# The banded attention of a hybrid encoder block: softmax issued behind the turned queries' copy in early slots, and a bank for transposed probabilities taken from the projections' ring

## The chip, the core and the metric

One core of a Trainium2 chip runs the whole kernel. TensorE (PE) does matrix products and transposes, ScalarE (ACT) activations and copies, VectorE (DVE) elementwise work and reductions, SyncE (SP) issues the DMAs. The metric is the device time of one execution in microseconds. Times of several executions are given by their median; the profile is of one further execution.

## What is computed

One encoder block on x of 1024 tokens and 1024 features, all in fp32. The change lies in branch B, attention within a window of 128 tokens, in blocks of 128 queries, 8 query heads on 2 key/value heads:

```python
h = rms_norm(x)
g_q, g_k, g_v, g_r, g_lr_f, g_lr_b, s_q, s_k, s_v, gate_a, gate_b = split(h @ w_in)
y_gla = gla_branch(...) @ w_o_gla                  # branch A, gated linear attention
q = rope(rms_norm(s_q)); k = rope(rms_norm(s_k))   # branch B
scores = q @ k.T * hd**-0.5, masked to |i - j| <= 128
m = maximum(scores.max(-1), sink)
p = exp(scores - m)
o = (p / (p.sum(-1) + exp(sink - m))) @ v
y_swa = o @ w_o_swa
x = x + (sigmoid(gate_a) * y_gla + sigmoid(gate_b) * y_swa) @ w_out
x = x + swiglu(rms_norm(x))
```

## The kernel before

A product in fp32 is made of three products of split operands (`mm3`, L73): each operand is a rounded high part and the rest, and high x high, high x low and low x high are summed in PSUM. So each operand has a copy on ACT (the high part, `...h`) and a subtraction on DVE (the low part, `...l`).

The kernel has three stretches: the first projections with the gated linear attention (to some 380 us), the banded attention beside projections (some 380 to 570 us), and the large products of the output and the feed-forward part (to the end, on PE almost alone). The change touches the second.

The second stretch runs in 22 time slots. The list `todo` gives each slot its stages; a unit n is one block of 128 queries of one key/value head (four query heads), 16 in all. The unit is prepared and rotated (`prep`, `a_rope`) around slot n+1, its queries are turned (`a_turn`) in slot n+2, scored in slot n+3 (`a_scores`, once for each of four heads), its probabilities transposed and split in slot n+4 (`a_probs`, for up to three key blocks) and multiplied with the values in slot n+5 (`a_out`). Within a slot the order is prep, a_rope, a_scores, a_turn, k_turn, a_out, a_probs. So slot t does the scores of unit t-3 and the turn of unit t-2, whose scores come in slot t+1.

`slot` emits the stages one after another, and after each it lets generators in the list `dense` emit a share of matmuls of other work (`fill`): first the projections (L73 with `wh`, `wl` and `xh`, `xl`; four accumulators at a time, whose results ACT scales and stores, L221 and L222), and, when these are used up, the first halves of later products (L246; two accumulators, which DVE scales, L249). When only the latter is left, `len(dense)` is 1.

PE runs in the order in which the code is written. The order on ACT, DVE and SP is set by a scheduler from the order in which instructions are emitted and from what they depend on; each of these queues then runs strictly in its order. PSUM has eight banks: four in the ring `mm` (`mmtile`: accumulators of projections and first halves) and four in the ring `ch` (`chtile`: scores, transposes, attention outputs). A tile of a ring takes the bank that was freed first, and its first writer waits until the last reader of that bank is done.

The steps that matter, by line: transposed queries `ch<-ident,qr` (L755), their copy `sqh` on ACT (L758) and rest `sql` on DVE (L759); scores `ch<-kTh,sqh` and the like (L73), with the mask and the row maximum on DVE (`p`, `mx`, L773); the softmax, which is emitted with the fourth head's scores: `mx`, `nm`, `es` on DVE (L780, L781, L783), `es` on ACT (L784), four exponentials on ACT (L787), `dn` and `rd` on DVE (L789, L791), four scales on ACT (L793); transposed probabilities `ch<-ident,p` (L804) with copy `ph` on ACT (L807) and rest `pl` on DVE (L808); the output copy `st<-ch` on ACT (L818), which four DMAs store (L820). Loads: `qr<-sq` (L716) and `kvr<-skv` (L722) on SP; `kvr` feeds the products of the key rotation on DVE (L695 to L698) and the values' split `vSh`, `vSl` (L731, L732).

Of the kernel before, what the change touches and what calls it, by code (L numbers as in the profile page):

```python
# [11 lines left out]
AF = mybir.ActivationFunctionType  # L12
ALU = mybir.AluOpType

P = 128
# [9 lines left out]
SF = ((2, 50), (9, 24), (18, 18), (1 << 30, 12))  # L25
# [5 lines left out]
def body(tc, i, out):  # L31
    nc = tc.nc
    with ExitStack() as root:
# [8 lines left out]
        def nm(s):  # L42
            uid[0] += 1
            return f"{s}_{uid[0]}"
# [4 lines left out]
        def chtile(shape, dt=F32):  # L49
            return psc.tile(list(shape), dt, tag="ch", name=nm("ch"))  # L50
# [24 lines left out]
        def mm3(o, ah, al, bh, bl, start, stop):  # L75
            mm(o, ah, bh, start, False)
            mm(o, ah, bl, False, False)
            mm(o, al, bh, False, stop)
# [177 lines left out]
        dense = []  # L256

        def fill(n):

            while n > 0 and dense:  # L260
                try:
                    next(dense[0])
                    n -= 1
                except StopIteration:
                    dense.pop(0)

        def share(plan, t):
            return next(n for end, n in plan if t < end)
# [5 lines left out]
        def slot(stages, n):  # L274

            stages = [f for f in stages if f]
            done = 0
            if not stages:
                fill(n)
            for j, f in enumerate(stages):  # L280
                f()
                t = n * (j + 1) // len(stages)
                fill(t - done)
                done = t
# [361 lines left out]
        with tc.manual_schedule(engines={mybir.EngineType.PE}):  # L646
            fill(44)
            for t in range(last + 1):
                work = [[at[t, j]] for j in (0, 5, 4, 3, 2, 1) if (t, j) in at]
                if t in behind:  # L650
                    work = work or [[]]
# [38 lines left out]
        keys, att = {}, {}  # L690
# [60 lines left out]
        def a_turn(g, n):  # L751
            a = att[g, n]
            qt = chtile((P, 4, P))
            for h in range(4):
                nc.tensor.transpose(qt[:, h], a.qn[:, h], ident)  # L755
            a.qh = sw.tile([P, 4, P], FR, tag="qh", name=nm("sqh"))
            a.ql = sw.tile([P, 4, P], FR, tag="ql", name=nm("sql"))
            nc.scalar.activation(a.qh, qt, AF.Copy)  # L758
            nc.vector.tensor_tensor(a.ql, qt, a.qh.bitcast(F32), op=ALU.subtract)  # L759
            a.b0, a.b1 = max(n - 1, 0), min(n + 1, KT - 1)  # L760
            a.w = (a.b1 - a.b0 + 1) * P

        def a_scores(g, n, h):
            a = att[g, n]
            if h == 0:
                a.p = sw.tile([P, 4, 384], F32, tag="p", name=nm("p"))
                a.mx = sw.tile([P, 4], F32, tag="mx", name=nm("mx"))
            w, p, mx = a.w, a.p, a.mx
            ks = slice(a.b0 * P, (a.b1 + 1) * P)
            mo = (a.b0 - (n - 1)) * P  # L770
            s = chtile((P, 384))
            mm3(s[:, :w], a.qh[:, h], a.ql[:, h], kTh[:, g, ks], kTl[:, g, ks], True, True)
            nc.vector.tensor_tensor_reduce(out=p[:, h, :w], in0=s[:, :w], in1=band[:, mo:mo + w],  # L773
                                           op0=ALU.add, op1=ALU.max, scale=1.0, scalar=-1e30,
                                           accum_out=mx[:, h:h + 1])
            if h < 3:
                return
            sk = sink[:, 4 * g:4 * g + 4]
            nm_ = sw.tile([P, 4], F32, tag="nm", name=nm("nm"))
            nc.vector.scalar_tensor_tensor(mx, mx, -1.0, a.rs, op0=ALU.mult, op1=ALU.mult)  # L780
            nc.vector.tensor_tensor(nm_, mx, nsink[:, 4 * g:4 * g + 4], op=ALU.min)  # L781
            es = sw.tile([P, 4], F32, tag="es", name=nm("es"))
            nc.vector.tensor_tensor(es, sk, nm_, op=ALU.add)  # L783
            nc.scalar.activation(es, es, AF.Exp)  # L784
            dn = sw.tile([P, 4], F32, tag="dn", name=nm("dn"))
            for h in range(4):
                nc.scalar.activation(p[:, h, :w], p[:, h, :w], AF.Exp, bias=nm_[:, h:h + 1],  # L787
                                     scale=a.rs[:, h:h + 1], accum_out=dn[:, h:h + 1])
            nc.vector.tensor_tensor(dn, dn, es, op=ALU.add)  # L789
            rd = sw.tile([P, 4], F32, tag="rd", name=nm("rd"))  # L790
            nc.vector.reciprocal(rd, dn)  # L791
            for h in range(4):
                nc.scalar.activation(p[:, h, :w], p[:, h, :w], AF.Copy, scale=rd[:, h:h + 1])  # L793

        def a_probs(g, n, kb):
            a = att[g, n]
            kb += a.b0
            if kb > a.b1:
                return
            if kb == a.b0:  # L800
                a.pts = []
            pt = chtile((P, 4, P))
            for h in range(4):
                nc.tensor.transpose(pt[:, h], a.p[:, h, (kb - a.b0) * P:(kb - a.b0 + 1) * P], ident)  # L804
            ph = sw.tile([P, 4, P], FR, tag="ph", name=nm("ph"), bufs=3)
            pl = sw.tile([P, 4, P], FR, tag="pl", name=nm("pl"), bufs=3)
            nc.scalar.activation(ph, pt, AF.Copy)  # L807
            nc.vector.tensor_tensor(pl, pt, ph.bitcast(F32), op=ALU.subtract)  # L808
            a.pts.append((kb, ph, pl))
# [24 lines left out]
        def xpart(q, k):  # L834
            r = xn.tile([P, HT], F32, tag="xn", name=nm("xn"))
            nc.sync.dma_start(out=r, in_=scr[f"x{q}", k])
            pool, th, tl, d = homes[q]
            XT[q].append(xsplit(pool, th.format(k + d), tl.format(k + d), r))
# [4 lines left out]
        for n in range(2 * KT):  # L843
            t, g = divmod(n, 2)
            todo[n + 5].append((a_out, g, t))
            todo[n + 4] += [(a_probs, g, t, kb) for kb in range(3)]
            todo[n + 3] += [(a_scores, g, t, h) for h in range(4)]
            todo[n + 2].append((a_turn, g, t))
            todo[n + 1].append((a_rope, g, t))
            if g == 0:  # L850
                todo[n + 1].append((prep, t))
                if t + 1 < KT:
                    todo[n + 2].append((k_turn, t + 1))
        order = (prep, a_rope, a_scores, a_turn, k_turn, a_out, a_probs)
        with tc.manual_schedule(engines={mybir.EngineType.PE}):
            for t, v in enumerate(todo):
                v.sort(key=lambda e: order.index(e[0]))
                if t > 2 * KT + 2 and v:
                    fill(8)
                slot([lambda e=e: e[0](*e[1:]) for e in v], share(SF, t))  # L860
                if t >= 2 * KT + 2:
                    assert len(dense) == 1
                    for q in ("T1", "22"):
                        xpart(q, t - 2 * KT - 2)
# [81 lines left out]
        def pair_T3(f):  # L946
            nme, m, a, b = PAIRS[f]
            g = pend[f]
            product(g.X, wsplit(g.s3, 512), XT["T3"], 4, False, True)
            return result((f"{nme}{m + 4}", 1), g.X, g.p5)  # L950
# [69 lines left out]
        with tc.manual_schedule(engines={mybir.EngineType.PE}):  # L1020
# [15 lines left out]
            for j in range(0, len(PAIRS), 2):  # L1036
# [4 lines left out]
                v = [pair_T3(f) for f in two]  # L1041
# [53 lines left out]
        def gate(nme, s):  # L1095
            g = bt.tile([P, HT], F32, tag=nme[:2], name=nm(nme[:2]))
            nc.sync.dma_start(out=g, in_=scr[nme, s])
            nc.scalar.activation(g, g, AF.Sigmoid)
            return g
# [119 lines left out]
        with tc.manual_schedule(engines={mybir.EngineType.PE}):  # L1219
# [29 lines left out]
            for m in (0, 4, 1, 5, 2, 6, 3, 7):  # L1249
                g = [gate(f"gb{m}", s) for s in range(2)]  # L1250
# [353 lines left out]
```

## Time and profile before

| | |
|---|---|
| median of three executions | 1626.66 us (1625.54 to 1628.33) |
| profiled execution | 1624.41 us |
| its span (first to last instruction) | 1622.6 us |
| PE busy | 1610.2 us (99%) |
| PE weight loads busy | 1339.9 us (83%) |
| DVE busy | 1222.0 us (75%) |
| ACT busy | 914.1 us (56%) |
| DMA | 323.26 MB, 198 GB/s over the span |

"Busy" is the share of the span in which an engine had an instruction running. PE's matmuls overlap, so their starts tell more than their lengths: where nothing holds PE, 512 columns follow each other every 0.23 us. In a timeline a row has the start and the duration in us, the engine, the line of the kernel, the operation, tiles written and read, and in brackets how long the engine stood idle before the row and which instruction released it.

### The profile page before, as it was taken

The page shows a single profiled execution, that of the slowest core. Times are in us where ns is not written, and L with a number is a line of the kernel's source. Part 1 is how long each engine was busy: PE and PEld are TensorE (multiplying, and loading weights), DVE is VectorE, ACT ScalarE, POOL GpSimd, SP SyncE. Part 2 cuts the span into 40 slices and gives each one's busy share as a digit, 9 for nine tenths or more (in the row PEclk, how much of TensorE's full clock was granted, in tenths as well). Part 3 has the DMA queues.
Part 4 walks back from the last instruction along what each step waited for, and adds up shares of the span by engine and source line. Part 5 has one row for each costly group of instructions (what it writes and reads, how often), then busy time and mean ns, then how long its engine had stood idle before and what let it go on. Part 6 is the DMA issues. An engine that isn't in the chain of part 4 may idle for free.

```text
span 1622.6 us, 23346 instructions
## 1 busy us (share of the span) xinstructions
PE 1610.2 (99%) x7628; PEld 1339.9 (83%) x7628; DVE 1222.0 (75%) x2307; ACT 914.1 (56%) x1875; POOL 0.2 (0%) x4
## 2 busy tenths in 40 slices
PE   9999999999999999999999999999999999999999
PEld 6888888888788888888888888888888888888887
DVE  8568888846899777876855878677777887789655
ACT  7455777863999745455633647754444444454442
POOL 0000000000000000000000000000000000000000
PEclk9999999999999999999999999999999999999999
DMA  8955757878554387878843656643435564695433
GB/s 272 306 180 187 254 191 242 274 264 279 170 173 143 105 283 257 271 237 261 286 120 95 192 196 210 196 141 123 137 120 178 168 220 145 209 332 186 149 98 117
DMA packets 197980, 323.26 MB, mean 199 GB/s; under 512 B 23423, under 2 KB 49919, under 8 KB 197858
## 3 DMA queue, kind: packets, MB, share of 16 engines
q1 hardware_dynamic: 197858, 321.77, 60.8%
q8 instruction: 60, 0.98, 0.3%
q14 instruction: 62, 0.51, 0.1%
HBM read 216.29 MB, written 105.39 MB: 198 GB/s over the span
## 4 chain that ended last, share of the span: by engine, by line
PE 85%; DVE 8%; ACT 4%; DMA 2%; issue 1%; SPq 0%; DVEq 0%; ACTq 0%
PE mm L73 16%; PE mm L898 10%; PE mm L900 10%; PE mm L899 10%; PE mm L1442 7%; PE ch L1442 6%; PE ch L898 5%; PE ch L900 5%; PE ch L899 5%; PE ch L73 5%; PE mm L246 4%; PE ch L804 1%; DMA kvr<-skv 1%; DVE wl L69 1%; DVE G L443 0%
## 5 line engine op out<-in xcount | busy, mean ns | idle before, releaser
L877 ACT ACTIVATE wh<-ws 128x512 fp32r<-128x512 f32 x164 | 103.1, 630 | 165.4 <-PE mm L899 85.8
L73 PE MATMUL mm<-wh,xl 128*128 128x512 f32 x320 | 127.2, 397 | 0.0
L73 PE MATMUL mm<-wl,xh 128*128 128x512 f32 x320 | 127.1, 397 | 0.0
L73 PE MATMUL mm<-wh,xh 128*128 128x512 f32 x320 | 126.6, 396 | 0.3 <-ACT lrt L313 0.3
L878 DVE TENSOR_TENSOR wl<-ws,wh 128x512 fp32r<-128x512 f32 x164 | 112.1, 685 | 15.4 <-ACT wh L877 14.9
L67 ACT ACTIVATE wh<-wr 128x512 fp32r<-128x512 f32 x114 | 70.8, 627 | 52.8 <-PE mm L73 20.0
L69 DVE TENSOR_TENSOR wl<-wr,wh 128x512 fp32r<-128x512 f32 x114 | 77.7, 684 | 22.5 <-ACT wh L67 21.3
L877 ACT ACTIVATE wh<-a 128x512 fp32r<-128x512 f32 x66 | 41.6, 632 | 89.6 <-PE ch L1442 42.3
L877 ACT ACTIVATE wh<-wr 128x512 fp32r<-128x512 f32 x76 | 48.0, 632 | 61.1 <-PE mm L899 19.9
L878 DVE TENSOR_TENSOR wl<-a,wh 128x512 fp32r<-128x512 f32 x66 | 45.3, 688 | 39.7 <-ACT wh L877 39.5
L73 PEld LDWEIGHTS mm<-wh,xh 128*128 128x128 f32 x320 | 60.2, 188 | 10.6 <-ACT lrt L313 0.7
L1442 PE MATMUL mm<-hh,wl 128*128 128x512 f32 x176 | 68.6, 390 | 0.0
L1442 PE MATMUL mm<-hh,wh 128*128 128x512 f32 x176 | 68.5, 389 | 0.0
L1442 PE MATMUL mm<-hl,wh 128*128 128x512 f32 x176 | 68.5, 389 | 0.0
L73 PEld LDWEIGHTS mm<-wl,xh 128*128 128x128 f32 x320 | 60.2, 188 | 9.7
L73 PEld LDWEIGHTS mm<-wh,xl 128*128 128x128 f32 x320 | 60.3, 188 | 9.0
L891 DVE TENSOR_TENSOR ws<-wr,wr 128x512 f32<-128x512 f32 x80 | 54.4, 684 | 7.1 <-DMA wr<-in_w_f_dram 3.2
L878 DVE TENSOR_TENSOR wl<-wr,wh 128x512 fp32r<-128x512 f32 x76 | 51.8, 683 | 7.0 <-ACT wh L877 6.4
L1409 DVE TENSOR_TENSOR hl<-hr,hh 128x512 fp32r<-128x512 f32 x77 | 52.6, 683 | 5.5 <-ACT hh L1408 5.4
L1408 ACT ACTIVATE hh<-hr 128x512 fp32r<-128x512 f32 x77 | 47.7, 619 | 8.5 <-DMA hr<-B 4.5
L73 PE MATMUL mm<-xl,wh 128*128 128x512 f32 x128 | 50.7, 396 | 0.7 <-DVE xl L330 0.7
L1442 PE MATMUL ch<-hh,wl 128*128 128x512 f32 x132 | 51.4, 389 | 0.0
(453 smaller groups left out, 4982.1 us busy)
## 6 DMA issues: line engine op xcount, KB each, us to landing
wr<-in_w_fi_dram SPq DMA_DIRECT2D x110, 256.0 KB, 3.8
wr<-in_w_f_dram SPq DMA_DIRECT2D x96, 256.0 KB, 3.5
wh<-wh SPq DMA_DIRECT2D x80, 256.0 KB, 3.0
wl<-wl SPq DMA_DIRECT2D x80, 256.0 KB, 3.1
B<-c SPq DMA_DIRECT2D x44, 256.0 KB, 2.1
T<-st SPq DMA_DIRECT2D x44, 256.0 KB, 2.9
a<-in_w_fo_dram SPq DMA_DIRECT2D x44, 256.0 KB, 5.3
hr<-T SPq DMA_DIRECT2D x44, 256.0 KB, 2.6
```

The costliest lines, as they stand in the source:

```text
L67: nc.scalar.activation(h, raw, AF.Copy)
L69: nc.vector.tensor_tensor(l, raw, h.bitcast(F32), op=ALU.subtract)
L73: nc.tensor.matmul(o, a, b, start=start, stop=stop)
L246: nc.tensor.matmul(Y[q], w[:, c], x, start=f0, stop=f1, skip_group_check=True)
L877: nc.scalar.activation(h, src, AF.Copy)
L878: nc.vector.tensor_tensor(l, src, h.bitcast(F32), op=ALU.subtract)
L891: nc.vector.tensor_tensor(t, x, y, op=op)
L898: nc.tensor.matmul(o, h[:, c], x[kk][0], start=start and kk == 0, stop=False, skip_group_check=True)
L899: nc.tensor.matmul(o, h[:, c], x[kk][1], start=False, stop=False, skip_group_check=True)
L900: nc.tensor.matmul(o, l[:, c], x[kk][0], start=False, stop=kk == nk - 1, skip_group_check=True)
L1409: nc.vector.tensor_tensor(l, r, h.bitcast(F32), op=ALU.subtract)
L1442: nc.tensor.matmul(ys[m], a[:, c], b, start=f0, stop=f1, skip_group_check=True)
```

## The change

Two edits. The first takes the softmax out of `a_scores` and emits it as a step of its own (`a_soft`, `a_exps`): in slots below 5 that also turn queries, behind the turn and with `tc.issue_after`, which holds the softmax's instructions behind ACT's copy of those queries (`turned[-1]`); in all other slots directly behind the slot's last scores, where it was. Scores begin in slot 3, so slots 3 and 4 are the ones in which the new place is used. The second edit takes the tile of the first key block's transposed probabilities from the ring `mm` instead of `ch`, as long as only the first halves are left in `dense`; this is so for twelve units. No instruction is added or removed, and PE's order is the same in both kernels but for the bank that those twelve groups write.

```diff
@@ -755,7 +755,7 @@
                 nc.tensor.transpose(qt[:, h], a.qn[:, h], ident)
             a.qh = sw.tile([P, 4, P], FR, tag="qh", name=nm("sqh"))
             a.ql = sw.tile([P, 4, P], FR, tag="ql", name=nm("sql"))
-            nc.scalar.activation(a.qh, qt, AF.Copy)
+            turned.append(nc.scalar.activation(a.qh, qt, AF.Copy))
             nc.vector.tensor_tensor(a.ql, qt, a.qh.bitcast(F32), op=ALU.subtract)
             a.b0, a.b1 = max(n - 1, 0), min(n + 1, KT - 1)
             a.w = (a.b1 - a.b0 + 1) * P
@@ -773,8 +773,16 @@
             nc.vector.tensor_tensor_reduce(out=p[:, h, :w], in0=s[:, :w], in1=band[:, mo:mo + w],
                                            op0=ALU.add, op1=ALU.max, scale=1.0, scalar=-1e30,
                                            accum_out=mx[:, h:h + 1])
-            if h < 3:
-                return
+
+        turned = []
+
+        def a_soft(g, n, pin):
+            a = att[g, n]
+            w, p, mx = a.w, a.p, a.mx
+            with tc.issue_after(turned[-1].ins) if pin else nullcontext():
+                a_exps(a, g, w, p, mx)
+
+        def a_exps(a, g, w, p, mx):
             sk = sink[:, 4 * g:4 * g + 4]
             nm_ = sw.tile([P, 4], F32, tag="nm", name=nm("nm"))
             nc.vector.scalar_tensor_tensor(mx, mx, -1.0, a.rs, op0=ALU.mult, op1=ALU.mult)
@@ -799,7 +807,7 @@
                 return
             if kb == a.b0:
                 a.pts = []
-            pt = chtile((P, 4, P))
+            pt = (mmtile if kb == a.b0 and len(dense) == 1 else chtile)((P, 4, P))
             for h in range(4):
                 nc.tensor.transpose(pt[:, h], a.p[:, h, (kb - a.b0) * P:(kb - a.b0 + 1) * P], ident)
             ph = sw.tile([P, 4, P], FR, tag="ph", name=nm("ph"), bufs=3)
@@ -857,7 +865,14 @@
                 v.sort(key=lambda e: order.index(e[0]))
                 if t > 2 * KT + 2 and v:
                     fill(8)
-                slot([lambda e=e: e[0](*e[1:]) for e in v], share(SF, t))
+                work = [[e] for e in v]
+                names = [e[0] for e in v]
+                if a_scores in names:
+                    pin = a_turn in names and t < 5
+                    k = names.index(a_turn) if pin else max(j for j, f in enumerate(names) if f is a_scores)
+                    g = v[names.index(a_scores)]
+                    work[k].append((a_soft, g[1], g[2], pin))
+                slot([lambda u=u: [f(*a) for f, *a in u] for u in work], share(SF, t))
                 if t >= 2 * KT + 2:
                     assert len(dense) == 1
                     for q in ("T1", "22"):
```

In the changed kernel the lines from L780 on are numbered 8 higher (L787 is L795, L804 is L812), and from the slots' loop on 15 higher. The scheduler's order of ACT and DVE differs in many places between 404 us and 570 us; the three that follow are those of the prediction. Tile names have running numbers.

ACT in slot 3 (`st` is a projection's result, `p` the probabilities of unit 0, `sqh` the copy of unit 1's turned queries that the next scores on PE read):

```order
 L221 ACTIVATE st_5473<-mm_5229,rstdt 128x512
-L787 ACTIVATE p_5401,dn_5448<-p_5401,nm_5442,rs_5201 128x256
-L784 ACTIVATE es_5445<-es_5445 128x4
-L787 ACTIVATE p_5401,dn_5448<-p_5401,nm_5442,rs_5201 128x256 x3
-L758 ACTIVATE sqh_5468<-ch_5463 128x512
+L758 ACTIVATE sqh_5450<-ch_5445 128x512
+L792 ACTIVATE es_5457<-es_5457 128x4
+L795 ACTIVATE p_5401,dn_5460<-p_5401,nm_5454,rs_5201 128x256 x4
 L221 ACTIVATE st_5495<-mm_5230,rstdt 128x512
-L793 ACTIVATE p_5401<-p_5401,rd_5454 128x256 x4
+L801 ACTIVATE p_5401<-p_5401,rd_5466 128x256 x4
```

The copy sqh moved ahead of es and the four exponentials; the next projection's store and the four scales stay behind them.

DVE at the same place:

```order
 L698 TENSOR_TENSOR qn_5615<-qn_5615,sq_5616 128x256
-L695 TENSOR_TENSOR rq_5627<-qr_5598,qB 128x4x64
-L789 TENSOR_TENSOR dn_5448<-dn_5448,es_5445 128x4
-L695 TENSOR_TENSOR rq_5627<-qr_5598,qB 128x4x64
-L791 RECIPROCAL rd_5454<-dn_5448 128x4
-L759 TENSOR_TENSOR sql_5469<-ch_5463,sqh_5468 128x512
+L759 TENSOR_TENSOR sql_5451<-ch_5445,sqh_5450 128x512
 L773 ISA p_5487,mx_5488<-ch_5489,band 128x256
 L773 ISA mx_5488 128x1
```

The split sql moved from behind dn and rd to right behind the key rotation's last row.

DVE where the scores of unit 5 begin (slot 8, around 450 us; `kvr` the loaded keys and values of a later block, `pl` the splits of unit 3's three transposed probabilities), before:

```order
L695 TENSOR_TENSOR sq_6508<-kvr_6494,kB 128x2x64 x2
L773 ISA p_6053,mx_6054<-ch_6055,band 128x384
L773 ISA mx_6054 128x1
L808 TENSOR_TENSOR pl_6014<-ch_6008,ph_6013 128x512
L808 TENSOR_TENSOR pl_6025<-ch_6019,ph_6024 128x512
L808 TENSOR_TENSOR pl_6040<-ch_6034,ph_6039 128x512
L773 ISA p_6053,mx_6054<-ch_6074,band 128x384
```

and after:

```order
L816 TENSOR_TENSOR pl_6014<-ch_6008,ph_6013 128x512
L695 TENSOR_TENSOR sq_6508<-kvr_6494,kB 128x2x64 x2
L773 ISA p_6053,mx_6054<-ch_6055,band 128x384
L773 ISA mx_6054 128x1
L773 ISA p_6053,mx_6054<-ch_6074,band 128x384
L773 ISA mx_6054 128x1
L816 TENSOR_TENSOR pl_6025<-ch_6019,ph_6024 128x512
```

The first pl moved ahead of the two products that read kvr, and the other two behind the second and third scores.

ACT in slot 18 (softmax of unit 15, `st` the output of unit 13, `ph` the copies of unit 14's probabilities), before:

```order
L787 ACTIVATE p_7484,dn_7516<-p_7484,nm_7510,rs_7084 128x256
L784 ACTIVATE es_7513<-es_7513 128x4
L787 ACTIVATE p_7484,dn_7516<-p_7484,nm_7510,rs_7084 128x256 x3
L818 COPY st_7540<-ch_7530 128x512
L807 ACTIVATE ph_7552<-ch_7547 128x512
L807 ACTIVATE ph_7575<-ch_7570 128x512
L793 ACTIVATE p_7484<-p_7484,rd_7522 128x256 x4
```

and after:

```order
L826 COPY st_7540<-ch_7530 128x512
L792 ACTIVATE es_7513<-es_7513 128x4
L795 ACTIVATE p_7484,dn_7516<-p_7484,nm_7510,rs_7084 128x256 x4
L815 ACTIVATE ph_7552<-mm_7547 128x512
L801 ACTIVATE p_7484<-p_7484,rd_7522 128x256 x4
L815 ACTIVATE ph_7575<-ch_7570 128x512
```

The copy st moved ahead of the exponentials, and the four scales between the first and the second ph. The first ph now reads a bank of the ring mm.

## The prediction

> **What bounds the kernel now.** I read the page first, then busy time by stage, then TensorE's waits by stage, and last the timelines around those waits. The page's first and fourth parts:
>
> ```profile
> PE 1610.2 (99%) x7628; PEld 1339.9 (83%) x7628; DVE 1222.0 (75%) x2307; ACT 914.1 (56%) x1875; POOL 0.2 (0%) x4
> ...
> PE 85%; DVE 8%; ACT 4%; DMA 2%; issue 1%; SPq 0%; DVEq 0%; ACTq 0%
> ```
>
> TensorE (PE) is busy 99% of the span and carries 85% of the chain that ended last. An average hides stages, so the same by stretch: window, its length, then busy us (and instructions) of PE, PEld, DVE, ACT and POOL, granted clock, DMA share, GB/s.
>
> ```profile
> 380.00:455.00 75.00, 71.37 (x369) 59.85 (x368) 58.86 (x175) 56.40 (x139) 0.00 (x0) 1.00 0.68 221
> 455.00:572.00 117.00, 116.69 (x633) 98.58 (x632) 101.22 (x280) 100.89 (x246) 0.00 (x0) 1.00 0.43 133
> 572.00:1200.00 628.00, 628.00 (x2771) 519.93 (x2770) 465.93 (x741) 326.01 (x564) 0.00 (x0) 1.00 0.61 197
> ```
>
> The change lies in the first two. From 572 on PE has no idle time at all, and the clock is 1.00, so what PE gains or loses before 572 arrives at the end unchanged. What can be gained is PE's waits there (us in total, times, longest), of the first window and, last row, of the second:
>
> ```profile
> PE ch L73 <- ACT sqh L758: 2.8, 1, 2.8
> PE ch L73 <- DVE mx L773: 0.7, 1, 0.7
> PE ch L73 <- DVE sql L759: 0.2, 1, 0.2
> ...
> PE ch L73 <- DVE mx L773: 0.2, 1, 0.2
> ```
>
> Under 4 us in all, so this is a change of a few us at most.
>
> **Part one, slot 3: the copy of turned queries goes ahead of the exponentials.** PE's, ACT's and DVE's timelines there (start, duration, line, tiles, idle before and its releaser):
>
> ```profile
> 403.31 0.60 PE L755 MATMUL ch<-ident,qr 128*128 128x128 f32 x4
> ...
> 404.68 0.39 PE L73 MATMUL mm<-wl,xh 128*128 128x512 f32 x1
> 404.91 0.40 PE L73 MATMUL mm<-wh,xl 128*128 128x512 f32 x1
> 408.06 0.39 PE L73 MATMUL ch<-kTh,sqh 128*128 128x256 f32 x1 [2.76 <-ACT sqh L758]
> ...
> 408.79 0.39 PE L73 MATMUL ch<-kTh,sql 128*128 128x256 f32 x1 [0.22 <-DVE sql L759]
> ```
>
> ```profile
> 403.82 0.67 ACT L221 ACTIVATE st<-mm,rstdt 128x512 f32<-128x512 f32 x1
> 404.99 0.60 ACT L787 ACTIVATE p<-p,nm,rs 128x256 f32<-128x256 f32 x1 [0.49 <-DVE nm L781]
> ...
> 407.44 0.57 ACT L758 ACTIVATE sqh<-ch 128x512 fp32r<-128x512 f32 x1
> 407.91 0.67 ACT L221 ACTIVATE st<-mm,rstdt 128x512 f32<-128x512 f32 x1
> 408.48 1.70 ACT L793 ACTIVATE p<-p,rd 128x256 f32<-128x256 f32 x4
> ```
>
> ```profile
> 405.21 0.15 DVE L783 TENSOR_TENSOR es<-sink,nm 128x4 f32<-128x4 f32 x1
> 405.28 0.42 DVE L698 TENSOR_TENSOR qn<-qn,sq 128x256 f32<-128x256 f32 x1
> ...
> 408.06 0.67 DVE L759 TENSOR_TENSOR sql<-ch,sqh 128x512 fp32r<-128x512 f32 x1
> ```
>
> The transposes end at 403.91. The copy sqh needs nothing else, yet ACT runs it at 407.44, behind four exponentials that it entered at 404.99. In the changed order it follows the store at 403.82, which holds ACT for 0.57 (407.91 to 408.48, the same form): sqh runs from 404.39 to 404.96. PE would arrive 0.23 after its 404.91 row, at 405.14, so the 2.8 us wait is gone. What is late next is sql on DVE, now behind es and qn: 405.28 + 0.34 (the row pitch of a 0.42 us operation: 0.42 less 0.08 overlap) = 405.62, and 0.67 long, 406.29; PE's third score matmul takes it 0.06 later (408.73 to 408.79 before), at 406.35. Unhindered it would start at 405.14 + 2 x 0.12 = 405.38 (256 columns at half the pitch of 0.23 that the 512-column rows show), so a new wait of about 0.97 appears. Gain: 408.79 - 406.35 = **2.44**. Upper bound, sql not late: 408.79 - 405.38 = 3.41. Lower bound 0: the copy as late as now. A loss in this part is excluded only as far as nothing behind the exponentials is late, and that is next.
>
> The four exponentials and es now start behind sqh and es on DVE (405.36), at 405.5, and end near 407.85; the store of st (L221) then starts at 407.85 against 407.91, and the four scales at 408.4 against 408.48. So they move by nothing on the clock, but PE stands 2.44 earlier. The scales end at 410.2; their reader (L804) stood at 413.95, now 411.5: covered by 1.3. The store's DMA on SP, and the three loads behind it (two weights and kvr), stay where they were:
>
> ```profile
> 410.00 0.38 SPq L722 DMA_DIRECT2D kvr<-skv  x1
> ```
>
> ```profile
> 414.54 0.42 ACT L723 ACTIVATE sq<-kvr 128x256 f32<-128x256 f32 x1 [0.26 <-DMA kvr<-skv]
> ```
>
> On DVE a product of kvr (L695) now stands ahead of the split pl of the first probabilities (L808), whose bank a score of slot 5 takes at 419.6, now 417.1. 414.5 + 0.3 + 0.7 = 415.5: covered by 1.6. I cost this part's other moves, L717 (1.06 us on ACT, now behind exponentials) and the splits of x, at nothing: their readers are the k turns and products several us away.
>
> **Part two, the score at 451.86.** PE's row, and the row before it:
>
> ```profile
> 450.81 0.40 PE L246 MATMUL mm<-xl,wh 128*128 128x512 f32 x1
> 451.86 0.44 PE L73 MATMUL ch<-kTh,sqh 128*128 128x384 f32 x1 [0.65 <-DVE mx L773]
> ```
>
> ```profile
> 450.84 0.49 DVE L695 TENSOR_TENSOR sq<-kvr,kB 128x128 f32<-128x128 f32 x2 [2.17 <-DMA kvr<-skv]
> ```
>
> The score could start at 450.81 + 0.23 = 451.04 and starts 0.82 late; its second matmul loses another 0.10. It waits for a ch bank that DVE frees in order, behind two products that wait 2.17 for kvr. In the new order pl of the first probabilities stands ahead of these products and frees a bank: ACT's copy ph lies before the scales and takes about 0.6, pl 0.7, and it is ready some 0.7 before PE asks. Gain **0.92**. The next score then hangs on mx behind kvr with about 0.3 to spare. Bounds: 0 (kvr 0.8 late or more) to 0.92.
>
> **Part three, the bank from the projections' ring.** From 459 to 566, twelve times, the first block's transposed probabilities no longer take one of the four ch banks. Before, six scores stand late for a ch bank there, the first and the last of them being:
>
> ```profile
> 492.69 0.40 PE L246 MATMUL mm<-xl,wh 128*128 128x512 f32 x1
> 493.00 0.44 PE L73 MATMUL ch<-kTh,sqh 128*128 128x384 f32 x1
> ...
> 546.28 0.40 PE L246 MATMUL mm<-xl,wh 128*128 128x512 f32 x1
> 546.83 0.38 PE L73 MATMUL ch<-kTh,sqh 128*128 128x256 f32 x1 [0.15 <-DVE mx L773]
> ```
>
> With a pitch of 0.23 these are 0.08 and 0.32 late; the others (494.31, 514.98, 535.59, 545.59), read the same way, 0.22, 0.20, 0.14 and 0.23, and each next matmul is 0.08 to 0.10 late too: 1.19 + 0.54 = 1.73. With a bank more, I take **1.65**; bounds 0 and 1.73. The four mm banks bear it: L246 holds two, and two are free.
>
> **Part four, a loss at the end.** ACT's order also changes in the last slots. Slot 18 now (the second fence is PE, at the start of slot 19):
>
> ```profile
> 558.96 0.60 ACT L787 ACTIVATE p<-p,nm,rs 128x256 f32<-128x256 f32 x1 [1.60 <-DVE nm L781]
> ...
> 561.40 0.56 ACT L818 COPY st<-ch 128x512 f32<-128x512 f32 x1
> 561.87 1.07 ACT L807 ACTIVATE ph<-ch 128x512 fp32r<-128x512 f32 x2
> 562.84 1.71 ACT L793 ACTIVATE p<-p,rd 128x256 f32<-128x256 f32 x4
> ```
>
> ```profile
> 559.37 0.39 PE L73 MATMUL ch<-ph,vSl 128*128 128x512 f32 x1
> ...
> 563.71 0.39 PE L73 MATMUL ch<-ph,vSh 128*128 128x512 f32 x1
> 563.94 0.39 PE L73 MATMUL ch<-pl,vSh 128*128 128x512 f32 x1
> ...
> 564.40 0.39 PE L73 MATMUL ch<-ph,vSh 128*128 128x512 f32 x1
> 564.63 0.39 PE L73 MATMUL ch<-pl,vSh 128*128 128x512 f32 x1
> ```
>
> After, the copy st stands first. It waits for the product that ends at 559.76, so the exponentials start at 560.37 instead of 558.96 and end (561.40 - 558.96 = 2.44 long) at 562.81. First ph to 563.38, its pl (0.67) to 564.05, which PE wants at 563.94: late by 0.15. Then the four scales, 1.71, before the second ph: 563.29 + 1.66 + 0.54 = 565.49, wanted at 564.40 + 0.15: late by 0.95. Its pl at 566.2, wanted at 564.63 + 1.10: late by 0.45 to 0.5. Sum 1.6, with 0.1 for the matmul behind a stall **1.7**. Slot 17 has the same new order, and by the same sum just fits (0.25). Bounds: 0 (the scheduler's order runs early because nm is early) and 3.4 (slot 17 too).
>
> **Sum.** -2.44 - 0.92 - 1.65 + 1.7 = -3.3. The profiled execution takes 1624.41, so about 1621.1; it stands 2.25 under the median of the runs, 1626.66, which gives **1623.4**. That is -0.20%, and 0.2% (3.25 us) is about what a measurement of this kernel can tell from no change.
>
> **Rivals.**
> - The tail fits. If slot 18's copies come in time, -5.0: 1621.7. For it: st and exponentials are both short. Against: the sum above leaves over a microsecond.
> - The first wait only changes its name. If DVE's rows ahead of sql stand later than now, or the two thin covers (0.3 at the second place, 0.25 in slot 17) fail, some 2.3 of the gain goes: -1.0, 1625.7. For it: sql is already the last to come in my own sum, and DVE is busy 101.22 of 117.
> - Slower: ACT's new order makes copies late in many slots. The price per slot is the 1.7 of slot 18; gains of 5.0 are used up from the third such slot on, and with four the time is 1626.66 - 5.0 + 6.8 = 1628.5; with five, 1630.2. For it: ACT is busy 100.89 of 117 and PE has no slack. Against: in the printed order only the last two put the scales between the first and the second ph.
> - PE is not the bound. A row for it is PEld, busy only 83%; then the removed waits return as other idle time, and the time stays 1626.7. Against it: PE has 628.00 of 628.00 from 572 on, and its matmuls there follow each other without a gap. [...]
>
> **How the numbers follow.** My sum 0.46 (it ends on the bound: faster 0.25, no difference 0.21); the tail fits 0.20 (faster); the first wait changes its name 0.20 (no difference); many late copies 0.10 (slower 0.08, no difference 0.02); PE not the bound 0.04 (no difference). Faster 0.45, same 0.47, slower 0.08. The range: all waits gone and no loss is -3.41 - 0.92 - 1.73 = -6.1, 1620.6; the upper end takes in the case of no effect, 1626.7, and leaves out the slower rival: 1620.5 to 1626.8.
>
> **What would show it.** In the changed profile the wait of PE for ACT's sqh is absent, a wait of some 0.9 for DVE's sql stands at 406; the wait at 451.86 (then near 448.6) and the small ones at 490 to 547 are gone; and between 558 and 562 PE waits twice or three times for ph and pl, 1.6 in all. I am wrong if sql comes by 405.4, if the late kvr (414.5, 448.2) passes its covers of 1.6 and 0.3, or if ph waits appear in more slots than 18.

## Result and profile after

The changed kernel takes 1621.67 us (median of 9 executions, 1621.26 to 1622.94) against 1626.66 us (9 executions, 1625.29 to 1628.33): ratio 0.9972, 95% interval [0.9962, 0.9982], or 2.9 to 6.2 us less (the ratio is not taken from the two medians, which alone would give 0.9969). Forecast were 1623.4 and -3.3. Its profiled execution took 1621.67, its own median, with a span of 1619.9; before's profiled execution, 1624.41, lay below all nine of its timed ones. Profile against profile the gain is 2.74; median against median 5.0. One later execution of before took 2821.80 us at a mean granted clock of 0.656; it is in no median, ratio or count below.

Page of the changed kernel, busy shares and chain:

```profile
PE 1609.6 (99%) x7628; PEld 1341.0 (83%) x7628; DVE 1223.6 (76%) x2307; ACT 914.7 (56%) x1875; POOL 0.2 (0%) x4
...
PE 90%; DVE 5%; ACT 2%; DMA 1%; issue 1%; SPq 0%; DVEq 0%; ACTq 0%
```

PE's share of the chain reads 90% where it read 85%. That share is no measure of the gain: the fastest variant below, with before's order in slot 18, has 87%. By stretch, and then PE's waits (first row of the first stretch, the others of the second):

```profile
380.00:455.00 75.00, 74.05 (x385) 62.67 (x384) 61.33 (x180) 57.78 (x143) 0.00 (x0) 1.00 0.68 221
455.00:572.00 117.00, 115.90 (x628) 98.43 (x627) 100.57 (x278) 101.58 (x247) 0.00 (x0) 1.00 0.45 139
```

```profile
PE ch L73 <- DVE sql L759: 0.8, 1, 0.8
...
PE ch L73 <- ACT ph L815: 0.8, 1, 0.8
PE ch L73 <- DVE pl L816: 0.2, 1, 0.2
```

PE's idle time before 455 went from 3.6 to 0.95 us; after 455 it went from 0.3 to 1.1. The wait for sqh is gone, one for sql is new, and so are those for ph and pl. Slot 4's first scores on PE, and ACT and DVE at the same place:

```profile
405.34 0.39 PE L73 MATMUL mm<-wh,xl 128*128 128x512 f32 x1
405.57 0.28 PE L73 MATMUL ch<-kTh,sqh 128*128 128x256 f32 x1
405.69 0.28 PE L73 MATMUL ch<-kTl,sqh 128*128 128x256 f32 x1
406.77 0.38 PE L73 MATMUL ch<-kTh,sql 128*128 128x256 f32 x1 [0.81 <-DVE sql L759]
```

```profile
404.70 0.59 ACT L758 ACTIVATE sqh<-ch 128x512 fp32r<-128x512 f32 x1
405.81 0.20 ACT L792 ACTIVATE es<-es 128x4 f32<-128x4 f32 x1 [0.52 <-DVE es L791]
```

```profile
405.70 0.42 DVE L698 TENSOR_TENSOR qn<-qn,sq 128x256 f32<-128x256 f32 x1
406.03 0.68 DVE L759 TENSOR_TENSOR sql<-ch,sqh 128x512 fp32r<-128x512 f32 x1
```

The first two matmuls follow the dense work without a gap; the third could start at 405.69 + 0.12 = 405.81 and comes 0.96 late. The score that stood late at 451.86, in the changed kernel (PE, and DVE's products of kvr):

```profile
448.70 0.39 PE L246 MATMUL mm<-xl,wh 128*128 128x512 f32 x1
448.93 0.33 PE L73 MATMUL ch<-kTh,sqh 128*128 128x384 f32 x1
```

```profile
447.92 0.48 DVE L695 TENSOR_TENSOR sq<-kvr,kB 128x128 f32<-128x128 f32 x2
```

No gap on PE. The end of slot 18, ACT and then PE:

```profile
555.45 0.59 ACT L826 COPY st<-ch 128x512 f32<-128x512 f32 x1 [1.68 <-PE ch L73]
555.93 0.21 ACT L792 ACTIVATE es<-es 128x4 f32<-128x4 f32 x1
556.04 0.59 ACT L795 ACTIVATE p<-p,nm,rs 128x256 f32<-128x256 f32 x1
...
558.38 0.58 ACT L815 ACTIVATE ph<-mm 128x512 fp32r<-128x512 f32 x1
558.98 1.71 ACT L801 ACTIVATE p<-p,rd 128x256 f32<-128x256 f32 x4
560.59 0.57 ACT L815 ACTIVATE ph<-ch 128x512 fp32r<-128x512 f32 x1
```

```profile
559.37 0.40 PE L73 MATMUL ch<-ph,vSh 128*128 128x512 f32 x1
559.74 0.50 PE L73 MATMUL ch<-pl,vSh 128*128 128x512 f32 x1
560.07 0.39 PE L73 MATMUL ch<-ph,vSl 128*128 128x512 f32 x1
561.22 0.49 PE L73 MATMUL ch<-ph,vSh 128*128 128x512 f32 x1 [0.76 <-ACT ph L815]
561.95 0.50 PE L73 MATMUL ch<-pl,vSh 128*128 128x512 f32 x1 [0.23 <-DVE pl L816]
```

With a pitch of 0.23, PE loses 0.14, 0.10, 0.92, 0.50 and 0.10 here: 1.8.

### The profile page after: what moved, and what is told of

Read it like the earlier page. It is cut to its first block, busy times and chain, and to the rows that moved or that the text cites. A ratio compares the mean times of both kernels' runs of the same rounds, so it can differ in the third digit from the quotient of the medians.

```text
span 1619.9 us, 23336 instructions
## 1 busy us (share of the span) xinstructions
PE 1609.6 (99%) x7628; PEld 1341.0 (83%) x7628; DVE 1223.6 (76%) x2307; ACT 914.7 (56%) x1875; POOL 0.2 (0%) x4
## 4 chain that ended last, share of the span: by engine, by line
PE 90%; DVE 5%; ACT 2%; DMA 1%; issue 1%; SPq 0%; DVEq 0%; ACTq 0%
PE mm L73 19%; PE mm L915 10%; PE mm L913 10%; PE mm L914 10%; PE mm L1457 7%; PE ch L73 7%; PE ch L1457 6%; PE ch L915 5%; PE ch L913 5%; PE ch L914 5%; PE mm L246 4%; PE ch L812 1%; DVE wl L69 0%; PE ch L755 0%; DVE G L443 0%
## 5 line engine op out<-in xcount | busy, mean ns | idle before, releaser
L1457 PE MATMUL ch<-hh,wh 128*128 128x512 f32 x132 | 51.3, 389 | 0.0
L1457 PE MATMUL ch<-hl,wh 128*128 128x512 f32 x132 | 51.3, 389 | 0.0
```

Source lines behind the costliest of these rows:

```text
L1457: nc.tensor.matmul(ys[m], a[:, c], b, start=f0, stop=f1, skip_group_check=True)
```

## Experiments

The numbers of the theory come from laying PE's matmuls of two profiles side by side in order, and taking the difference of their starts. Ratios are against executions of before in the same round; its medians in the three rounds were 1626.93, 1626.35 and 1626.70 us. The first four ran together.

**Only the first edit.** `pt = chtile((P, 4, P))` kept, the softmax moved.

```diff
-            pt = (mmtile if kb == a.b0 and len(dense) == 1 else chtile)((P, 4, P))
+            pt = chtile((P, 4, P))
```

> Only the first edit (the softmax behind the turned queries' copy in slots 3 and 4); the transposed probabilities stay in the ring ch. Theory: the two edits add up. The printed order of ACT and DVE up to 455 us is that of the full change, so the wait of 2.9 in slot 3 becomes one of 0.96 for sql (-2.5 with the matmul behind it) and the wait of 0.9 at 451.9 goes: -3.4 us against before, 1623.2; the small waits between 490 and 547 stay, and the 1.8 us of waits in slot 18 are absent. Rival: the measured -5.0 is more than the sum of -3.3 because before loses more in slots 3 to 8 than its one profile shows; then this edit alone gives the whole -5.0, 1621.7.

1621.42 us, ratio 0.9972 [0.9961, 0.9983]: the whole gain. The theory's number (1623.2) was missed, the rival's was met. All six executions lay between 1620.96 and 1622.56.

**Only the second edit.**

```diff
-            pt = chtile((P, 4, P))
+            pt = (mmtile if kb == a.b0 and len(dense) == 1 else chtile)((P, 4, P))
```

> Only the second edit (the first key block's transposed probabilities in the ring mm); the softmax stays where it was. Theory: the small waits for ch banks go (-1.7), and the loss in slot 18 (+1.8) and a wait of 0.36 in slot 18's scores belong to this edit: +0.5 us against before, 1627.1, no difference that can be told. The wait for sqh at 408 (2.9) stays. Rival: the order in slot 18 is the doing of the softmax's new place; then this edit gives -1.7, 1625.0, and no waits for ph in slot 18.

1627.55 us, ratio 1.0004 [0.9996, 1.0013]; waits of PE after 455:

```profile
PE ch L73 <- ACT ph L807: 0.8, 1, 0.8
PE ch L73 <- DVE mx L773: 0.7, 1, 0.7
PE ch L73 <- DVE pl L808: 0.2, 1, 0.2
```

The wait for ph is here without the first edit: the loss in slot 18 belongs to the bank, which takes what it gives. The softmax's new place does not cause it.

**The changed kernel with before's order in slot 18.**

```diff
+            with tc.issue_after(exped[-1].ins) if 2 * n + g in (13,) else nullcontext():
-            nc.scalar.copy(ob, o)
+                nc.scalar.copy(ob, o)
```

(`exped` collects each unit's last exponential.)

> The full change, with ACT's copy of unit 13's output held behind the exponentials of unit 15 in slot 18, which restores before's order there (exponentials, st, ph, ph, then the scales). Theory: the 1.8 us that PE loses in slot 18 for ph and pl are due to that order alone and nothing takes their place: 1.8 under the full change, 1619.9, and no PE wait for ph. Rival: the copies are late for another cause (a busy ACT), or the next wait takes their place: within 0.5 of the full change, 1621.7.

1620.15 us, ratio 0.9964 [0.9952, 0.9977], the fastest median of this study; the interval overlaps that of the full change, so the order of the two rests on the trace. PE there:

```profile
559.21 0.40 PE L73 MATMUL ch<-ph,vSh 128*128 128x512 f32 x1
559.47 0.50 PE L73 MATMUL ch<-pl,vSh 128*128 128x512 f32 x1
559.80 0.40 PE L73 MATMUL ch<-ph,vSl 128*128 128x512 f32 x1
560.04 0.39 PE L73 MATMUL ch<-ph,vSh 128*128 128x512 f32 x1
560.27 0.40 PE L73 MATMUL ch<-pl,vSh 128*128 128x512 f32 x1
```

The two long stalls are gone and nothing takes their place: side by side with the full change, PE gains 1.6 at these rows, and the two profiles end 1.65 apart. The order was the cause.

**Before, a second profile.** No edit.

> The kernel before, once more, for a second profile. Ratio 1.000. The profiled execution of before was 1624.4, 2.3 under its median. Theory: executions differ in waits that hang on DMAs landing (kvr, qr) between 380 and 455 us; this profile shows 1625 to 1628 and more waits of PE there than 4.7 us. Rival: a profiled execution is shorter than a timed one of this kernel by some 2 us whatever it waits for; then 1624.4 again with the same waits.

1626.81 us, ratio 0.9999 [0.9990, 1.0008]; the profiled execution took 1626.81. Neither side had it right. The waits are those of the first profile (sqh 2.7, mx 0.5, sql 0.2). What differs stands behind the wait for sqh:

```profile
405.60 0.40 PE L73 MATMUL mm<-wh,xl 128*128 128x512 f32 x1
408.74 0.39 PE L73 MATMUL ch<-kTh,sqh 128*128 128x256 f32 x1 [2.74 <-ACT sqh L758]
...
410.99 0.63 PE L73 MATMUL mm<-wh,xl 128*128 128x512 f32 x1
411.42 0.63 PE L73 MATMUL mm<-wh,xh 128*128 128x512 f32 x1
411.84 0.63 PE L73 MATMUL mm<-wl,xh 128*128 128x512 f32 x1
...
413.33 0.39 PE L73 MATMUL mm<-wh,xh 128*128 128x512 f32 x1
413.56 0.28 PE L73 MATMUL ch<-kTh,sqh 128*128 128x256 f32 x1
```

512 columns take 0.43 where they took 0.23 before and after. By single microseconds (the third number from the end is the granted clock), this profile and, last, the first profile of before:

```profile
408.00:409.00 1.00, 0.26 (x2) 0.26 (x2) 0.76 (x4) 1.00 (x4) 0.00 (x0) 1.00 0.89 250
409.00:410.00 1.00, 0.78 (x5) 0.53 (x5) 0.52 (x2) 1.00 (x4) 0.00 (x0) 0.95 0.77 293
410.00:411.00 1.00, 1.00 (x6) 0.91 (x5) 0.32 (x2) 0.90 (x4) 0.00 (x0) 0.50 1.02 293
412.00:413.00 1.00, 1.00 (x6) 0.90 (x5) 0.00 (x0) 0.01 (x1) 0.00 (x0) 0.50 0.91 268
413.00:414.00 1.00, 1.00 (x7) 0.87 (x7) 0.85 (x3) 0.00 (x0) 0.00 (x0) 0.84 0.66 252
```

```profile
410.00:411.00 1.00, 1.00 (x7) 0.86 (x7) 0.43 (x2) 0.19 (x2) 0.00 (x0) 1.00 0.93 262
```

The clock is halved for some 3.4 us behind the idle time, and PE falls back 1.55 (side by side with the first profile, it is 0.68 late ahead of this stretch and 2.23 behind it). The profile that the prediction was made from is one in which it was not halved. That is a new theory, and the next runs test it: the idle time costs its length and in most executions also a stretch at half clock.

**Idle time filled.** Useless matmuls ahead of slot 4's first score, nothing else changed in the code. There were 12, 4 and later 24 of them. With 4 and 12 the traces show before's order on ACT, DVE and SP through the second stretch; with 24 a few steps of ACT and DVE stand in another order between 413 and 424 us.

```diff
             s = chtile((P, 384))
+            if (g, n, h) == (1, 0, 0):
+                for _ in range(12):
+                    nc.tensor.matmul(s[:, :w], kTh[:, g, ks][:, 0:P], kTh[:, g, ks], start=True, stop=True)
             mm3(s[:, :w], a.qh[:, h], a.ql[:, h], kTh[:, g, ks], kTl[:, g, ks], True, True)
```

> The kernel before, with 12 useless matmuls of 256 columns (1.4 us) on PE directly ahead of the first score of slot 4, into that score's own bank, which the score then overwrites. The order of ACT, DVE and SP is that of before. The copy sqh that PE waits for is no earlier, so PE's idle time there shrinks from 2.8 to 1.4 us and the score starts when it did. Theory: in most executions of before the granted clock falls to 0.50 for 3.4 us after that idle time, which costs 1.6 us; the shorter idle time leaves the clock at 1.00: 1625.2, 1.7 under before, clock 1.000 in nearly all executions. Rival: the clock falls for another reason (or the extra time of before is in DMA waits); then 1626.9 as before, with 0.50 in some microseconds after 409.

> As the run before, with 4 such matmuls (0.5 us), so that 2.3 us of idle time are left. [...] Rival (clock not tied to the idle time): 1626.9.

> The kernel of the run idle_filled once more, for a second profile. There the clock stayed at 1.00 in 9 of 11 executions, yet these were 1.3 slower than before's executions at 1.00; the one profile put 0.8 of that on kvr, which landed 0.8 later. Theory: kvr's landing varies from execution to execution (4.4 to 5.3 us in the profiles so far), and PE's wait at 452 takes up much of what is won in slot 4: again 1.000 in most executions, 1625.8, and a wait at 452 between 0.5 and 1.6. Rival: the useless matmuls themselves cost something at a fixed place; then the profile shows a step at another place, the same in both.

> As idle_filled with 24 useless matmuls (2.8 us), so that PE hardly idles ahead of slot 4's scores, whose start stays where sqh puts it (408 to 408.3). Theory: the clock is 1.000 in all executions, and the time is that of idle_filled's executions at 1.000, 1625.3 to 1625.8. Rival: executions with less than 1.000 are as frequent as with 12 matmuls, since the idle time is not their cause.

> The kernel before, for a third profile. Theory: the clock at 0.50 for some 3.4 us after the idle time in slot 4 (as in the second profile), since 5 of 60 executions so far had 1.000; time 1625.5 to 1628; the wait at 452 between 0.5 and 1.6 with kvr landing 4.4 to 5.3 after its issue. Rival: 1.00 throughout as in the first profile.

Each execution has a mean granted clock, to three places. It can fall below 1.000 without cost too, at the end of the span where PE has finished (the profile with before's order in slot 18, at 0.999, is at half clock only from 1616.6 us on, and PE ends at 1614.6). So it marks slot 4 only roughly; the dependence on the idle time is strong all the same. Two kernels of the last two rows (slot 3 alone, slots 17 and 18) follow below:

| kernel | PE idle in slot 4 | executions at 1.000 | their median | median of the others |
|---|---|---|---|---|
| before (all 96 executions with a clock on record) | 2.7 to 3.1 us | 8 of 96 | 1624.55 | 1626.48 at 0.999, 1627.72 at 0.998 |
| 4 useless matmuls | 2.5 | 4 of 11 | 1625.03 | 1626.96 |
| 12 | 1.0 and 1.3 | 9 of 11 and 8 of 11 | 1625.75, 1626.12 | 1628.3, 1628.0 |
| 24 | 0 | 11 of 11 | 1625.97 | none |
| full change | 0.8 | 9 of 9 | 1621.67 | none |
| second edit alone | 3.4 | 2 of 11 | 1626.41 | 1627.55 at 0.999, 1628.49 at 0.998 |
| first edit alone; slot 3 alone | 0.4; 0.8 | 6 of 6; 11 of 11 | 1621.42; 1622.84 | none |
| slot 18, slots 17 and 18 in before's order | 0.8; 0.4 | 3 of 5; 4 of 5 | 1620.36; 1620.26 | 1620.05; 1620.65 |

Before once more took 1627.01, ratio 0.9999 [0.9990, 1.0009], as the theory has it. This third profile has the half clock longer still, from just before 408 to 414.6, some 6.8 us; two of them:

```profile
408.00:410.00 2.00, 1.50 (x4) 1.22 (x5) 1.33 (x5) 2.00 (x5) 0.00 (x0) 0.50 0.87 326
```

and PE falls back 2.45 there. With 12 matmuls the same stretch is at full clock:

```profile
410.00:412.00 2.00, 2.00 (x14) 1.72 (x13) 0.75 (x5) 1.06 (x2) 0.00 (x0) 1.00 0.98 344
```

So the clock follows the idle time: shown. Among the executions of before and of the kernels with 4 and 12, those at 1.000 are 1.9 to 2.55 us faster than those at 0.999; with the second edit alone it is 1.1. Where the idle time was 0.8 or less, the few executions at 0.999 are no slower beyond the scatter. The theories were right about the clock. But the kernels' medians did not fall as expected: 1626.25 and 1626.72 with 12, ratios 1.0002 [0.9993, 1.0011] and 1.0001 [0.9992, 1.0010]; 1626.88 with 4, 1.0001 [0.9992, 1.0009]; 1625.97 with 24, 0.9995 [0.9986, 1.0004]. At 1.000, those with 12 and 24 are 1.2 to 1.6 slower than before at 1.000. The first profile with 12 has the difference at one place, the score that waits behind kvr:

```profile
451.82 0.49 DVE L695 TENSOR_TENSOR sq<-kvr,kB 128x128 f32<-128x128 f32 x2 [2.98 <-DMA kvr<-skv]
```

```profile
452.85 0.44 PE L73 MATMUL ch<-kTh,sqh 128*128 128x384 f32 x1 [1.46 <-DVE mx L776]
```

kvr landed 5.3 us after its issue (446.49) instead of 4.5, and PE waits 0.8 longer; in the second profile 4.9, and 0.4 longer; with 24, 3.3, and PE waits 0.3 less there, though two later scores lose 0.6 and 0.3 to late splits pl. So part of what slot 4 wins, the old order gives back at the next wait. Why kvr lands later there in two of three profiles stays open, and with it the rest of the 1.2 to 1.6. What the half clock costs is therefore read from the traces (0.43 against 0.23, 1.55 and 2.45 in all) and not from these medians, which do not show it.

**Slots 17 and 18 in before's order.** `(13,)` above becomes `(12, 13)`.

> The full change with ACT's copies of the outputs of units 12 and 13 both held behind the exponentials (slots 17 and 18 in before's order). Theory: beyond the 1.5 that slot 18 gave, the wait of 0.27 (and 0.10 behind it) of a score at 551.7 for DVE's mx goes, which comes from slot 17's order: 1619.8, against 1620.15 with slot 18 alone. Rival: slot 17 cost nothing that is not waited elsewhere: 1620.15.

1620.6 us, ratio 0.9963 [0.9951, 0.9976]: the rival. The score that stood 0.27 late for mx now stands 0.20 late for pl.

**Only slot 3.** `t < 5` becomes `t < 4`, probabilities in ch.

> Of the first edit only slot 3 (the bound 5 becomes 4); probabilities in the ring ch. Theory: slot 3 holds the one wait that is worth anything, and DVE's new order at 450 us comes with it: 1621.4 as with slots 3 and 4. Rival: the second slot's new place brings the order at 450: then the wait there (0.9) is back, 1622.3.

1622.84 us, ratio 0.9976 [0.9967, 0.9985], against 1621.42 with both slots. The wait at 450 is not back, so the theory's place is right, but not its number. PE's waits before and after 455 name what the second slot's place is worth:

```profile
PE ch L73 <- ACT kTh L742: 0.2, 1, 0.2
...
PE ch L812 <- ACT st L826: 0.3, 1, 0.3
```

A turned key's copy and an output's copy come late, 0.8 and 0.5 with the matmuls behind them; neither wait stands in the profile with both slots. The intervals overlap, and the two ran in different rounds, so the 1.4 between the medians rests on this reading (the two profiles are 1.4 apart as well).

## Why the prediction was right in its terms and short in its size

Before and after, PE's starts side by side, against the terms of the sum:

| step | predicted | first profiles |
|---|---|---|
| slot 3, sqh ahead, new wait for sql | -2.44 | -2.94 - 0.11 + 0.58 = -2.47 |
| score at 451.86 | -0.92 | -0.93 (and -0.08 at a score at 440) |
| six scores late for a ch bank | -1.65 | -1.68 |
| slot 18, ph and pl late | +1.7 | +1.78 |
| score in slot 18 late for mx | none | +0.36 |
| ahead of the change (kTl at 399, start) | none | +0.45 |
| together | -3.31 | -2.57 |

The two profiles end 2.74 apart; the rest comes in small steps behind slot 18.

- The wait that takes over, 0.97 for sql, was measured at 0.96. DVE runs sql behind es and qn, as the prediction had it.
- The work that stayed at its place while PE moved up did no harm, as said: kvr's scores in slot 5 and the probabilities of unit 0 show no wait.
- The bank was costed right on both sides: the run with only the second edit shows that its gain and its loss are one edit's, and the run with before's order in slot 18 that the loss comes from the order on ACT. Part of the bank's gain comes without it: with the first edit alone four small waits of 0.2 stand after 455, not six with 1.73 in all.
- Not foreseen: 0.36 in slot 18, a score waiting for the row maximum of another (its bank). It stands in the run with only the second edit too, so it belongs to that edit; before's order in slots 17 and 18 takes little of it, and its cause stays open.
- What was mis-sized is the last step, "it stands 2.25 under the median": the difference of two profiles was carried over to the medians unchanged. That holds only where both kernels' executions differ from their profiles by the same amount. Before's do by 2.1 (1626.66 against 1624.55 at a clock of 1.000); the changed kernel's, by nothing. The removed wait was 2.9 long by the profile and cost a half clock besides, 1.55 and 2.45 in the two profiles of before that show it.
- That the half clock is what was missing shows in a second pair. Side by side with the second profile of before, which took that kernel's median, the changed kernel ends 5.15 earlier: the table's steps from slot 3 on (2.8 here), 1.55 for the half clock, 0.26 ahead of slot 3, and the rest in small steps, most of them behind slot 18.
- The measured 1621.67 is the number of the rival "The tail fits" (1621.7), but not its mechanism: slot 18's copies came 1.78 late. That the two numbers meet is chance.
- The case "PE is not the bound" is out: the gain of PE's stretch before 572 arrived at the end, with PEld still at 83%.

In windows of 2 us up to 1616 us, the granted clock of six profiles (the first two of before, the full change, each edit alone, and before's order in slot 18) is 1.00 throughout, but for one stretch at 0.50 near 410 us in the second profile of before and in that of the second edit alone. Four of the thirteen profiles have such a stretch behind the wait for sqh. By the mean clocks of single microseconds it lasts from 409.9 to 413.3 us in the second profile of before, from 409.6 to 413.0 with the second edit alone, from 408.3 to 411.7 with 4 useless matmuls, and from 407.8 to 414.6 in the third profile of before: 3.4 us three times and 6.8 once. PE had waited 2.7, 3.4, 2.5 and 3.1 us. In the first profile of before it waited 2.76 and the clock stayed at 1.00; so it did in seven other profiles, with waits of 1.3 or less. What sets the first profile of before, with 2.76 us, apart from the second, with 2.74, was not shown. The runs show only that it is rare: 8 of 96 executions of before have a mean clock of 1.000.

## What to carry to other kernels

In this kernel 2.5 to 3.4 us of idle TensorE had a stretch at half clock behind it in four of five profiles (3.4 us, once 6.8) and none in the fifth. An idle time of that size is to be priced with a possible stretch at half clock, and whether it comes can differ from one execution to the next. So look at the granted clock there in more than one profile before a gain is sized. One profile below all timed executions is a warning: find what the others have and it has not. And when a list scheduler sorts again, read its order at the far end of the stretch too: the bank's gain at 493 to 547 us was lost in slot 18, at 560, by one copy that moved ahead of four exponentials.

## What was not expected of the hardware

- 2.74 us of idle TensorE had 3.4 us at half clock behind it in one profile of before, and 2.76 had none in another; in the third, with 3.1 us idle, the half clock lasted 6.8; 512 columns then took 0.43 instead of 0.23 us.
- How often the clock stays at 1.000 goes with the idle time in slot 4: 2 of 11 executions with 3.4 us, 8 of 96 with 2.7 to 3.1, 4 of 11 with 2.5, 17 of 22 with 1.0 and 1.3, 11 of 11 with none.
- A DMA of 256 KB (kvr) took 3.3 to 5.3 us from issue to landing at the same place in the program.
